# Reordering the first feed-forward groups of an encoder block, and its last stores

## The chip, the cores and the metric

One Trainium2 chip, one of its cores. The metric is the time of one execution on the device in microseconds, the median of several runs; lower is better. Five engines work side by side, each through its own instruction queue in order: PE (TensorE, matmuls), DVE (VectorE), ACT (ScalarE), POOL (GpSimd), and SP (SyncE), which here only issues DMA transfers. ACT also issues a few transfers.

## The reference

One layer of a hybrid encoder over 1024 tokens of width 1024, all in float32: an input LayerNorm, one wide projection, dilated attention and a bidirectional gated recurrence, their gated merge, and then the part that matters here.

```python
h = layer_norm(DEEPNORM_ALPHA * h + merged @ w_o[l], ln1_g[l], ln1_b[l])
gate, up = jnp.split(h @ w_ffn_in[l], 2, axis=-1)          # 1024 -> 2 x 2816
h = layer_norm(DEEPNORM_ALPHA * h + (jax.nn.silu(gate) * up) @ w_ffn_out[l], ln2_g[l], ln2_b[l])
```

## The kernel before

**Precision.** A float32 product is made of three matmuls (`mm3`): both factors are split into a high part (a rounding cast on ACT, L204) and a low part (the difference, on POOL or DVE, L208), and hi x hi, hi x lo and lo x hi are summed in PSUM (L229 to L231). A matmul on a weight block therefore needs a cast and a difference first; the split blocks (`w_hi`, `w_lo`) lie in a ring of four.

**Winograd-Strassen groups.** Products of the feed-forward part are computed in 2 x 2 blocks with seven block products instead of eight. Of the weights, the raw block columns `f_raw` hold a11, a12, a21, a22; s1 to s4 are sums of them. Of the activations, h is cut into blocks b11, b12, b21, b22 of 4 x 128 rows by 512 tokens; t1 to t4 are sums of them:

```python
PRODUCTS = {5: ("s1", "t1"), 1: ("a11", "b11"), 2: ("a12", "b21"), 6: ("s2", "t2"), 3: ("s4", "b22"),
            7: ("s3", "t3"), 4: ("a22", "t4")}
```

A group has one pair of raw blocks and seven products of 12 matmuls of 128x512 each. There are 22 groups; partial sums are kept by ACT (`wkeep`, "keep") or left in PSUM, and four evictions (`evac` in `ffn_in`) turn them into the tile `fc`: for the first row a DVE add (L1447), a tanh on ACT (L1448) and a DVE product (L1449).

**The passage from w_o to the groups (`phase2`).** Eight tiles of 128 tokens pass through w_o, in two halves of 512 columns each (`half(t, 0)`, `half(t, 1)`: 24 matmuls, then DVE's residual add L1227 into the row `y1` and its statistics). `norm` normalises the row (ACT, for tile 7 DVE L1239; the inverse root is a power on POOL, L1235). `turn(t)` transposes it on PE (L259), evicts it (`tsv`), makes the sums for the blocks (`h1_blocks`) and stores the row. Tiles 0 to 3 give b11 and b21; tiles 4 to 7 give t1 and t2, which stay on chip, and b22, t3 and t4, which DVE makes in `tsum` tiles and SP stores to the scratch `td` in memory (L1307) because their place is still taken. `ffn_in` loads those three "late blocks" from `td` (`t_raw`, L1504) and splits them, four pieces each.

From tile 7 to the end of the first two groups the order on every engine is written by hand: inside `in_order()` each instruction is bound behind the one emitted before it on its engine. The two first groups g0 and g1 run as generators (`wino_ahead`) that `phase2` and `ffn_in` advance in turns. Everything else is ordered by a planner that picks what is ready. On-chip memory of a closed pool is used again by later pools; an instruction that writes there waits for the last use of the tile that lay there.

**The output product (`ffn_out`).** The same seven products for `w_ffn_out`, with 11 block steps each; in the last product but one, p = 7, the activations `ghi`, `glo` (from scratch `gs3`) are loaded three steps ahead by SP, inside a hand-written order in which also the finished rows 0 to 3 are normalised (`whole`, `end`) and stored. Then the last product runs by token tile t = 0 to 3 over `a22h`, `a22l`, two tiles of which are loaded ahead and two when their buffers come free.

Of the kernel before, what the change touches and what calls it, by code (L numbers as in the profile page):

```python
# [10 lines left out]
F32 = mybir.dt.float32  # L11
# [3 lines left out]
OP = mybir.AluOpType  # L15
# [63 lines left out]
TABW = 128 * 5 + 64 + 256 + 384 + 256 + 192  # L79


class Block:
# [171 lines left out]
    def transposed(self, pool, n, q, g, b, v=None, bufs=2, on_act=(1, 3, 6)):  # L254
# [887 lines left out]
    def phase2(self):  # L1142
        nc = self.nc
        gc, bc = self.col["g1"], self.col["b1"]
        with ExitStack() as es:
# [56 lines left out]
            def load(t):  # L1202
                Y[t] = yp.tile([128, D], F32, name="y1", tag="y1", bufs=3)
                nc.sync.dma_start(Y[t], self.ahs_d[t])
# [45 lines left out]
            for t in range(7):  # L1250
# [11 lines left out]
                if t < 6:  # L1262
                    turn(t)()
# [5 lines left out]
            self.lasts = {}  # L1269
            with self.in_order():  # L1270
                half(7, 0)
                rest = turn(6)
                self.first_groups = [self.wino_ahead(raws[f], lambda *a, f=f: self.first_evac[f](*a), f)
                                     for f in range(2)]
# [16 lines left out]
    def h1_blocks(self, pool, t, v, last=False):  # L1291
# [9 lines left out]
        if t < 4:  # L1301
            for i, n in enumerate(("b11", "b21")):
                put(n, v(i))
            return lambda: None
# [18 lines left out]
        def rest():  # L1323
            nc.vector.tensor_sub(t2, b22, t1)
            put("t2", t2)
            t3 = tmp()
            nc.vector.tensor_sub(t3, b22, b12)
# [5 lines left out]
            nc.vector.tensor_add(t4, t4, lo)  # L1333
            later(2, "t4", t4)

        return rest

    def wino_a(self, A, name):

        nc = self.nc  # L1340
        how = {"s1": ("a21", "a22", OP.add, nc.vector), "s2": ("s1", "a11", OP.subtract, nc.vector),
               "s3": ("a11", "a21", OP.subtract, nc.gpsimd), "s4": ("a12", "s2", OP.subtract, nc.vector)}
        if name not in A:
            a, b, op, e = how[name]
            A[name] = o = A["sum"]()
            e.tensor_tensor(o, A[a], A[b], op)  # L1346
        return A[name]

    def wino_parts(self, raws, evac, swap):

        nc = self.nc
        A = {"sum": lambda: self.ws.tile([128, 4, 128], F32, name="wsum", tag="wsum", bufs=3)}
        for i, r in enumerate(raws):
            for j in range(2):
                A[f"a{i + 1}{j + 1}"] = r[:, 4 * j:4 * j + 4, :]
        banks, made = {}, {}

        def prep(n):
            hi, lo = made[n] = self.granules()
            self.split(hi, lo, self.wino_a(A, self.PRODUCTS[n][0]))  # L1360

        def product(n, bank, first):
            if n not in made:
                prep(n)
            hi, lo = made[n]
            xhi, xlo = self.xb[self.PRODUCTS[n][1]]
            if first:
                banks[bank] = self.ps_pj() if (bank == 2) != swap else self.ps_sd()
            ps = banks[bank]
            for k in range(4):  # L1370
                self.mm3(ps, hi[:, k, :], lo[:, k, :], xhi[:, k, :], xlo[:, k, :], first and k == 0, k == 3,
                         skip_group_check=True)
            return ps

        def keep(ps):
            with self.tc.high_priority(offset=self.evac_ahead):
                t = self.ws.tile([128, HALF], F32, name="wkeep", tag="wkeep", bufs=4)
                nc.scalar.copy(t, ps)
            return t

        def out(i, l, ps, add):
            with self.tc.high_priority(offset=self.evac_ahead):
                evac(i, l, ps, add)

        return prep, product, keep, out

    def wino_project(self, raws, evac):

        prep, product, keep, out = self.wino_parts(raws, evac, False)
        m5 = keep(product(5, 2, True))  # L1390
        yield
        m1 = keep(product(1, 1, True))
        out(0, 0, product(2, 3, True), m1)
        u2 = keep(product(6, 1, False))
        out(0, 1, product(3, 2, False), u2)
        out(1, 1, product(7, 1, False), m5)
        yield
        out(1, 0, product(4, 1, False), None)

    def wino_ahead(self, raws, evac, f):  # L1400

        prep, product, keep, out = self.wino_parts(raws, evac, f == 1)
        prep(1)
        prep(2)
        yield
        m1 = keep(product(1, 1, True))
        c11 = product(2, 3, True)
        prep(5)
        yield
        out(0, 0, c11, m1)  # L1410
        prep(6)
# [18 lines left out]
    def ffn_in(self):  # L1430

        nc = self.nc
        with ExitStack() as es:
# [75 lines left out]
            with self.in_order():  # L1509
# [8 lines left out]
                for f in splits[4:]:  # L1518
                    f()
# [359 lines left out]
```

## Time and profile before

| | us |
|---|---|
| median of 3 runs | 2172.78 |
| lowest and highest | 2172.17, 2176.0 |
| profiled execution, its own time | 2176.61 |
| span of that execution, first to last instruction | 2174.8 |
| PE busy | 2046.9 (94%) |
| DVE busy | 1392.7 (64%) |
| POOL busy | 1200.0 (55%) |
| ACT busy | 916.1 (42%) |

The page of the profile tells the busy time of each engine, the chain of work that ended last and the costliest groups of instructions. Other views of the trace list the instructions of one engine in order of time with the idle time before them in brackets and what ended it, or the busy time of all engines in stretches of the span. Lines are named by their line in the kernel (L208); `fc<-wkeep,sd` reads "writes `fc` from `wkeep` and `sd`", where `sd` and `pj` are PSUM banks. Times are counted from the start of the span.

### The profile page before, as it was taken

Reading aid. Unit: us, or ns where it says so; the run is one execution under the profiler, and the core shown is the slowest. Engines: PE = TensorE matmul, PEld = TensorE weight load, DVE = VectorE, ACT = ScalarE, POOL = GpSimd, SP = SyncE. Lnnn points to the kernel's source line nnn. Section 1 sums busy time; section 2 is a strip of 40 time slices with the busy share of each in tenths; the row PEclk is TensorE's granted clock in tenths of the full one; section 3 lists DMA queues with packets and bytes.
Section 4 is the critical chain, followed back from the end, with each engine's and each line's share of the span. In section 5 each row is a group of like instructions: output and inputs, shape, how many; then the busy total and the mean of one; then the engine's idle time right before and its main releaser. Section 6 shows DMA issues by size and latency. Waiting matters only on the chain. (4 is left out here: it accounts for less than half of the span.)

```text
span 2174.8 us, 31264 instructions
## 1 busy us (share of the span) xinstructions
PE 2046.9 (94%) x10941; PEld 1682.7 (77%) x10941; DVE 1392.7 (64%) x2172; ACT 916.1 (42%) x1867; POOL 1200.0 (55%) x955
## 2 busy tenths in 40 slices
PE   4799999999999999989999899996999999999987
PEld 3678887778878888778888688784788888888866
DVE  7667646876368845867455623445668787868645
ACT  6534455434544436344363421243444434344221
POOL 3565553566436764656545764232567776754552
PEclk9899999999999999999999999998999999999999
DMA  5343442435334352334526663434434454458664
GB/s 205 101 127 101 154 142 85 143 115 158 122 108 140 124 170 93 122 117 135 163 94 207 224 229 115 126 107 131 131 127 163 155 170 155 146 204 289 204 224 140
DMA packets 296447, 324.20 MB, mean 149 GB/s; under 512 B 15905, under 2 KB 212834, under 8 KB 296290
## 3 DMA queue, kind: packets, MB, share of 16 engines
q1 hardware_dynamic: 288832, 296.81, 42.3%
q10 hardware_dynamic: 7458, 25.40, 2.9%
q8 instruction: 86, 1.41, 0.3%
q14 instruction: 71, 0.58, 0.1%
HBM read 211.78 MB, written 110.36 MB: 148 GB/s over the span
## 5 line engine op out<-in xcount | busy, mean ns | idle before, releaser
L208 POOL TENSOR_TENSOR w_lo<-wa,w_hi 128x512 fp32r<-128x512 f32 x276 | 386.4, 1408 | 275.4 <-ACT w_hi L204 261.5
L204 ACT CAST w_hi<-wa 128x512 fp32r<-128x512 f32 x276 | 170.0, 618 | 231.7 <-PE pj L230 167.8
L208 POOL TENSOR_TENSOR w_lo<-wsum,w_hi 128x512 fp32r<-128x512 f32 x88 | 134.2, 1534 | 97.3 <-ACT w_hi L204 62.0
L208 POOL TENSOR_TENSOR w_lo<-f_raw,w_hi 128x512 fp32r<-128x512 f32 x66 | 108.5, 1656 | 69.7 <-ACT w_hi L204 66.1
L229 PE MATMUL pj<-xt1hi,w_hi 128*128 128x512 f32 x268 | 107.8, 403 | 12.6 <-ACT xt1hi L204 6.8
L230 PE MATMUL pj<-xt1lo,w_hi 128*128 128x512 f32 x268 | 106.6, 398 | 4.5 <-DVE xt1lo L208 4.5
L231 PE MATMUL pj<-xb22hi,w_lo 128*128 128x512 f32 x268 | 104.8, 391 | 1.9 <-POOL w_lo L208 1.9
L231 PE MATMUL pj<-xt1hi,w_lo 128*128 128x512 f32 x268 | 106.2, 396 | 0.0
L229 PE MATMUL pj<-xb22hi,w_hi 128*128 128x512 f32 x268 | 105.7, 394 | 0.0
L230 PE MATMUL pj<-xb22lo,w_hi 128*128 128x512 f32 x268 | 104.8, 391 | 0.0
L463 POOL TENSOR_TENSOR wa<-wa,wa 128x512 f32<-128x512 f32 x46 | 64.4, 1402 | 71.2 <-DVE ws L462 56.2
L208 POOL TENSOR_TENSOR w_lo<-Wb,w_hi 128x512 fp32r<-128x512 f32 x47 | 65.2, 1388 | 68.2 <-ACT w_hi L204 68.2
L208 POOL TENSOR_TENSOR w_lo<-ws,w_hi 128x512 fp32r<-128x512 f32 x46 | 67.3, 1466 | 63.1 <-ACT w_hi L204 60.9
L204 ACT CAST w_hi<-wsum 128x512 fp32r<-128x512 f32 x88 | 54.6, 621 | 74.1 <-PE sd L230 57.5
L485 ACT COPY wkeep<-pj 128x512 f32<-128x512 f32 x138 | 80.2, 581 | 11.4 <-DVE evh L377 5.9
L229 PE MATMUL pj<-xt2hi,w_hi 128*128 128x512 f32 x188 | 76.2, 406 | 8.5 <-ACT w_hi L204 8.5
L229 PE MATMUL pj<-xb11hi,w_hi 128*128 128x512 f32 x188 | 77.9, 416 | 5.2 <-DVE wkeep L402 3.0
L1448 ACT ACTIVATE fth<-fc 128x512 f32<-128x512 f32 x44 | 27.8, 632 | 126.4 <-DVE fc L1447 126.4
L388 DVE TENSOR_TENSOR evh<-wkeep,pj 128x512 f32<-128x512 f32 x48 | 32.7, 680 | 75.1 <-PE pj L231 54.8
L229 PE MATMUL pj<-xt4hi,w_hi 128*128 128x512 f32 x188 | 75.9, 404 | 4.0 <-DVE evh L377 4.0
L231 PE MATMUL pj<-xt2hi,w_lo 128*128 128x512 f32 x188 | 75.6, 402 | 3.7 <-POOL w_lo L208 3.5
L975 ACT ACTIVATE hS<-hR,dec 128x128 f32<-128x128 f32 x112 | 44.5, 402 | 79.8 <-DVE hR L984 57.2
(423 smaller groups left out, 6689.7 us busy)
## 6 DMA issues: line engine op xcount, KB each, us to landing
wa<-in_w_in_dram SPq DMA_DIRECT2D x184, 256.0 KB, 3.0
f_raw<-in_w_ffn_in_dram SPq DMA_DIRECT2D x44, 512.0 KB, 4.0
Wb<-in_w_ffn_out_dram SPq DMA_DIRECT2D x40, 256.0 KB, 5.2
tg<-evh SPq DMA_DIRECT2D x32, 256.0 KB, 3.2
tg<-tg SPq DMA_DIRECT2D x16, 512.0 KB, 4.0
y<-ahs SPq DMA_DIRECT2D x16, 512.0 KB, 5.9
ah<-xt ACTq DMA_DIRECT2D x8, 512.0 KB, 6.5
rec<-hg ACTq DMA_DIRECT2D x8, 512.0 KB, 3.9
```

Of the source, the lines that this page charges most:

```text
L204: nc.scalar.copy(hi, src)
L208: e.tensor_sub(lo, src, hi.bitcast(F32))
L229: nc.tensor.matmul(ps, whi, xhi, start=first, stop=False, **kw)
L230: nc.tensor.matmul(ps, whi, xlo, start=False, stop=False, **kw)
L231: nc.tensor.matmul(ps, wlo, xhi, start=False, stop=last, **kw)
L388: nc.vector.tensor_add(t, add, ps)
L463: nc.gpsimd.tensor_sub(a["a21"], a["a11"], a["a21"])
L485: nc.scalar.copy(t, ps)
L975: nc.scalar.activation(S[:, c, :], E, AF.Copy, scale=dec[:, 1, c:c + 1])
L1448: nc.scalar.activation(th[:, s], c[:, s], AF.Tanh, scale=0.5)
```

## The change

Five things change.

- The first two groups are objects of a class `Group` with single steps instead of generators. Weight blocks are prepared at least a product ahead: g0's s1, s2 and the splits for products 1 and 2 stand before w_o half (7, 0), g1's for 1 and 2 behind half (7, 1), and so on.
- `turn` now returns two parts. The second (t2) and the rest (b22, t3, t4) are placed separately: the rests of tiles 6 and 7 stand together behind g1's products 1 and 2.
- The late blocks are split at other places: b22 behind g1's product 6, t3 behind g0's product 3, t4 behind g1's product 3.
- Sums are made in place: s3 and s4 overwrite a11 and a12 in `f_raw`, t3 overwrites b12, t4 overwrites t2. `y1` has 2 buffers (3 before) and `tsv` 4 (2 before).
- In `ffn_out` the stores of finished rows are put in a list and issued in the loop of the last product, behind the loads for it.

The diff, cut to its core:

```diff
+class Group:
+    HOW = {"s1": ("a21", "a22", OP.add, "vector"), "s2": ("s1", "a11", OP.subtract, "vector"),
+           "s3": ("a11", "a21", OP.subtract, "gpsimd"), "s4": ("a12", "s2", OP.subtract, "vector")}
+    def sum(self, name):
+        if name not in A:
+            a, b, op, e = self.HOW[name]
+            if name in ("s1", "s2"):
+                A[name] = o.ws.tile([128, 4, 128], F32, name="wsum", tag="wsum", bufs=3)
+            else:
+                A[name] = A[a]
+            getattr(o.nc, e).tensor_tensor(A[name], A[a], A[b], op)
+        return A[name]
+    def first(self):
+        self.m1 = self.keep(self.product(1, 1, True))
+        self.c11 = self.product(2, 3, True)
+    ...
 # phase2
-                Y[t] = yp.tile([128, D], F32, name="y1", tag="y1", bufs=3)
+                Y[t] = yp.tile([128, D], F32, name="y1", tag="y1", bufs=2)
 ...
             with self.in_order():
+                g0.sum("s1")
+                g0.sum("s2")
+                g0.prep(1, 2)
                 half(7, 0)
-                rest = turn(6)
-                self.first_groups = [...]
-                next(self.first_groups[0])
+                second, rest = turn(6)
                 half(7, 1)
                 norm(7)
+                g1.prep(1, 2)
+                second()
+                g0.first()
+                second, last = turn(7)
+                g0.prep(5)
+                second()
+                g1.first()
+                g0.prep(6)
                 rest()
-                next(self.first_groups[0])
-                next(self.first_groups[1])
-                turn(7)()
+                last()
 # h1_blocks
-        def rest():
+        def second():
             nc.vector.tensor_sub(t2, b22, t1)
             put("t2", t2)
-            t3 = tmp()
-            nc.vector.tensor_sub(t3, b22, b12)
-            later(1, "t3", t3)
+        def rest():
             later(0, "b22", b22)
-            t4 = tmp()
+            nc.vector.tensor_sub(b12, b22, b12)
+            later(1, "t3", b12)
             hi, lo = (z[:, :, c].bitcast(F32) for z in self.xb["b21"])
-            nc.vector.tensor_sub(t4, hi, t2)
-            nc.vector.tensor_add(t4, t4, lo)
-            later(2, "t4", t4)
+            nc.vector.tensor_sub(t2, hi, t2)
+            nc.vector.tensor_add(t2, t2, lo)
+            later(2, "t4", t2)
 # ffn_in
             with self.in_order():
+                g0.out(0, 0, g0.c11, g0.m1)
+                g0.m5 = g0.keep(g0.product(5, 2, True))
+                g1.prep(5)
+                g0.u2 = g0.keep(g0.product(6, 1, False))
+                g1.out(0, 0, g1.c11, g1.m1)
+                g1.prep(6)
                 splits = late_block(0)
-                next(g1)
+                g1.m5 = g1.keep(g1.product(5, 2, True))
+                g0.prep(3)
                 splits += late_block(1)
-                next(g0)
+                g1.u2 = g1.keep(g1.product(6, 1, False))
                 for f in splits[:4]:
                     f()
-                next(g1)
-                nxt = self.ffn_raws(FS[2])
+                g0.prep(7)
+                g0.out(0, 1, g0.product(3, 2, False), g0.u2)
                 for f in splits[4:]:
                     f()
+                g1.prep(3)
                 splits = late_block(2)
-                next(g0)
+                g0.out(1, 1, g0.product(7, 1, False), g0.m5)
+                g1.prep(7)
+                g1.out(0, 1, g1.product(3, 2, False), g1.u2)
+                g0.prep(4)
                 for f in splits:
                     f()
-                next(g1)
-                next(g0, None)
+                nxt = self.ffn_raws(FS[2])
+                g1.out(1, 1, g1.product(7, 1, False), g1.m5)
+                g0.out(1, 0, g0.product(4, 1, False), None)
 # ffn_out
             def end():
                 t = ends.pop(0)
                 nc.vector.tensor_add(Y[t], Y[t], V[1])
-                store(t)
+                stores.append(t)
 ...
                     if t < 2:
                         for i in range(2):
                             last_acts(2 + t, i)
+                    while stores:
+                        store(stores.pop(0))
```

More of the change, by code (lines that the diff above doesn't have):

```diff
@@ L79, with __init__, prep, product @@
 TABW = 128 * 5 + 64 + 256 + 384 + 256 + 192
+class Group:
+    HOW = {"s1": ("a21", "a22", OP.add, "vector"), "s2": ("s1", "a11", OP.subtract, "vector"),
+           "s3": ("a11", "a21", OP.subtract, "gpsimd"), "s4": ("a12", "s2", OP.subtract, "vector")}
+    def __init__(self, block, raws, swap=False):
+        self.o, self.swap, self.evac = block, swap, None
+        self.A = {f"a{i + 1}{j + 1}": r[:, 4 * j:4 * j + 4, :] for i, r in enumerate(raws) for j in range(2)}
+        self.banks, self.made = {}, {}
+    def sum(self, name):
+        A, o = self.A, self.o
+        if name not in A:
[6 more added lines that the diff above has]
+        return A[name]
+    def prep(self, *ns):
+        for n in ns:
+            hi, lo = self.made[n] = self.o.granules()
+            self.o.split(hi, lo, self.sum(self.o.PRODUCTS[n][0]))
+    def product(self, n, bank, first):
+        o = self.o
+        if n not in self.made:
+            self.prep(n)
+        hi, lo = self.made.pop(n)
+        xhi, xlo = o.xb[o.PRODUCTS[n][1]]
+        if first:
+            self.banks[bank] = o.ps_pj() if (bank == 2) != self.swap else o.ps_sd()
+        ps = self.banks[bank]
+        for k in range(4):
+            o.mm3(ps, hi[:, k, :], lo[:, k, :], xhi[:, k, :], xlo[:, k, :], first and k == 0, k == 3,
+                  skip_group_check=True)
+        return ps
+    def keep(self, ps):
+        o = self.o
+        with o.tc.high_priority(offset=o.evac_ahead):
+            t = o.ws.tile([128, HALF], F32, name="wkeep", tag="wkeep", bufs=4)
+            o.nc.scalar.copy(t, ps)
+        return t
+    def out(self, i, l, ps, add):
+        with self.o.tc.high_priority(offset=self.o.evac_ahead):
+            self.evac(i, l, ps, add)
+    def first(self):
+        self.m1 = self.keep(self.product(1, 1, True))
+        self.c11 = self.product(2, 3, True)
+    def steps(self, evac):
+        self.evac = evac
+        self.m5 = self.keep(self.product(5, 2, True))
+        yield
+        self.first()
+        self.out(0, 0, self.c11, self.m1)
+        self.u2 = self.keep(self.product(6, 1, False))
+        self.out(0, 1, self.product(3, 2, False), self.u2)
+        self.out(1, 1, self.product(7, 1, False), self.m5)
+        yield
+        self.out(1, 0, self.product(4, 1, False), None)
@@ L1262, in phase2 @@
                 if t < 6:
-                    turn(t)()
+                    for f in turn(t):
+                        f()
                 else:
@@ L1303, in h1_blocks @@
                 put(n, v(i))
-            return lambda: None
+            return ()
         def later(i, name, v):
@@ L1336, in h1_blocks @@
[L1336 to L1411, printed above, removed]
-        m5 = keep(product(5, 2, True))
-        u2 = keep(product(6, 1, False))
-        prep(3)
-        prep(7)
-        yield
-        out(0, 1, product(3, 2, False), u2)
-        out(1, 1, product(7, 1, False), m5)
-        yield
-        out(1, 0, product(4, 1, False), None)
+            nc.vector.tensor_sub(t2, hi, t2)
@@ L1422, in ffn_raws @@
+            nc.vector.tensor_add(t2, t2, lo)
+            later(2, "t4", t2)
+        return second, rest
     def ffn_raws(self, f):
@@ L1736, in whole @@
                     end()
-            ends = []
+            ends, stores = [], []
             def end():
```

13 lines of the change are left out of this document (7 added, 6 removed).

## The prediction

> **What bounds the kernel now.** I read the stages of TensorE first (busy time of each engine in stretches), then who TensorE waited for, then the order of time of each engine where it waits.
>
> ```profile
> 1388.30:1476.40 88.10, 86.82 (x409) 71.50 (x407) 45.11 (x95) 35.98 (x65) 28.27 (x29) 1.00 0.36 113
> 1476.40:1546.50 70.10, 46.40 (x152) 34.21 (x152) 36.30 (x57) 24.71 (x48) 19.07 (x15) 0.81 0.36 117
> 1546.50:1934.00 387.50, 386.69 (x1692) 316.55 (x1692) 307.19 (x288) 162.97 (x288) 279.19 (x175) 1.00 0.47 155
> 2104.00:2130.00 26.00, 13.26 (x36) 9.57 (x36) 12.76 (x21) 8.77 (x11) 16.59 (x11) 0.74 0.40 142
> ```
>
> Columns: stretch, length, busy time of PE, PEld, DVE, ACT, POOL, granted clock, DMA share, GB/s. The w_o halves before 1476 and the feed-forward loop after 1546 are full of matmuls: time saved ahead of the loop stays saved. TensorE is short of work in two places, the first groups (1476 to 1546) and the end of `ffn_out` (from 2104). The change touches both. What TensorE waits for in the first place, and the speed at which it resumes:
>
> ```profile
> 1479.65 0.50 PE L229 MATMUL sd<-xb11hi,w_hi 128*128 128x512 f32 x1 [3.34 <-ACT w_hi L204]
> 1492.08 0.79 PE L231 MATMUL pj<-xb11hi,w_lo 128*128 128x512 f32 x1 [1.83 <-POOL w_lo L208]
> 1505.69 0.80 PE L229 MATMUL sd<-xt2hi,w_hi 128*128 128x512 f32 x1 [4.27 <-ACT w_hi L204]
> 1511.05 0.63 PE L231 MATMUL sd<-xt2hi,w_lo 128*128 128x512 f32 x1
> 1511.48 0.63 PE L229 MATMUL sd<-xt1hi,w_hi 128*128 128x512 f32 x1
> 1523.11 0.79 PE L229 MATMUL pj<-xt2hi,w_hi 128*128 128x512 f32 x1 [8.45 <-ACT w_hi L204]
> 1534.05 0.50 PE L229 MATMUL sd<-xt3hi,w_hi 128*128 128x512 f32 x1 [2.14 <-ACT xt3hi L204]
> 1546.50 0.50 PE L229 MATMUL sd<-xt4hi,w_hi 128*128 128x512 f32 x1 [1.25 <-ACT w_hi L204]
> ```
>
> The brackets are idle time. Matmuls start 0.43 us apart behind the longer pauses (1511.05, 1511.48); in the loop one takes 386.69 / 1692 = 0.228. Twelve products and one set of transposes are 12 x 12 x 0.228 + 1.0 = 33.9 us of full-speed work; they lie between 1476.3 and 1545.25, 68.9 us. So 35 us are to be had: 23.7 idle by the stage's row, the rest slow clock.
>
> **The change, part by part.** *Weights a product ahead.* The casts of g0's products 1 and 2 move ahead of w_o half (7,0), so g0's first 24 matmuls follow half (7,1) at 1476.3 and end at 1481.8. Tile 7's transposes are next, and they need its normalised row:
>
> ```profile
> 1470.88 0.68 DVE L1227 SCALAR_TENSOR_TENSOR y<-pj,y 128x512 f32<-128x512 f32 x1
> 1478.33 0.68 DVE L1227 SCALAR_TENSOR_TENSOR y<-pj,y 128x512 f32<-128x512 f32 x1
> 1479.73 2.51 POOL L208 TENSOR_TENSOR w_lo<-f_raw,w_hi 128x512 fp32r<-128x512 f32 x2 [13.52 <-ACT w_hi L204]
> 1480.02 0.15 DVE L1234 TENSOR_SCALAR mv<-mv 128x1 f32<-128x1 f32 x1
> 1482.19 0.55 POOL L1235 TENSOR_TENSOR mv<-mv,mhalf 128x1 f32<-128x1 f32 x1
> 1482.78 1.00 DVE L1239 TENSOR_SCALAR y<-y,mv 128x512 f32<-128x512 f32 x2 [2.61 <-POOL mv L1235]
> 1464.84 1.03 PE L259 MATMUL sd<-tabs_sb,y 128*128 128x128 f32 x8
> y<-ahs SPq DMA_DIRECT2D x8, 512.0 KB, 5.9
> ```
>
> The power on POOL stood behind the two w_lo of g0; these are now done earlier, so it starts at 1480.2 and not 1482.19. Against that stands `y1` with 2 buffers: tile 7's row can only be loaded when tile 5's transposes have read theirs (1465.87), and lands 0.3 + 5.9 us later, at 1472.1 or sooner; its use at 1470.88 slips by about 0.9 (0 if the load is faster). Half (7,1) is then evicted at 1479.2, the power ends at 1481.7, the row at 1482.7, the transposes at 1483.9, and g1's 24 matmuls, whose weights were prepared in the meantime, at 1489.3. The waits of 3.34 and 1.83 and the slow stretches behind them are gone. The other deeper or shallower rings (`tsv`, `tsum`) cost nothing: tile 7's slots were last used for tile 5's sums and tile 6's first one, which are done by then.
>
> *Late sums of tile 6 behind tile 7's.* This is where the next wait arises:
>
> ```profile
> 1488.45 1.37 DVE L269 TENSOR_SCALAR tsv<-sd,vc 128x128 f32<-128x128 f32 x4 [0.15 <-PE sd L259]
> 1496.05 0.69 DVE L208 TENSOR_TENSOR xt2lo<-tsum,xt2hi 128x512 fp32r<-128x512 f32 x1 [0.69 <-ACT xt2hi L204]
> 1496.66 0.69 DVE L1327 TENSOR_TENSOR tsum<-tsv 128x512 f32<-128x512 f32 x1
> 1497.98 0.69 DVE L1333 TENSOR_TENSOR tsum<-tsum,xb21lo 128x512 f32<-128x512 f32 x1
> 1502.25 0.69 DVE L1447 TENSOR_TENSOR fc<-wkeep,sd 128x512 f32<-128x512 f32 x1 [2.98 <-DMA td<-tsum]
> ```
>
> g0's first eviction (`fc`) waits until tile 7's last sum t4 has been stored, because `fc` is laid where `tsum` was; 3.6 us pass from that sum's end to `fc`. The order after keeps this wait and puts six sums, not three, ahead of it. DVE after 1482.7: tile 6's t2 pair as before (2.0), tile 7's evictions to xt2lo 1488.45 to 1496.74, of which I take 7.6 (POOL runs against it for less of the time), six sums at 2.0 for three: 1496.4; `fc` at 1500.0. In the DVE order g1's s1 stands behind this `fc`, and so do s2 and all later sums; ACT's tanh stands there too, ahead of g1's casts. From `fc` to the first matmul on the sum's cast took 1502.25 to 1505.69, 3.44. So g1's product 5 starts at 1503.4. TensorE covers until about 1497 with g0's products 5 and 6 (their own short waits are swallowed by this): 6.4 idle, then 1.3 for w_lo and ten matmuls at 0.43, to 1508.8. Product 6 follows without a wait, to 1511.6: the 8.45 is gone.
>
> *Late blocks behind the sixth products.*
>
> ```profile
> 1511.72 0.59 ACT L1378 COPY wkeep<-sd 128x512 f32<-128x512 f32 x1 [5.59 <-PE sd L231]
> L1448 ACT ACTIVATE fth<-fc 128x512 f32<-128x512 f32 x44 | 27.8, 632 | 126.4 <-DVE fc L1447 126.4
> 1515.97 2.17 ACT L204 CAST xb22hi<-t_raw 128x512 fp32r<-128x512 f32 x4
> 1535.44 0.50 PE L230 MATMUL sd<-xt3lo,w_hi 128*128 128x512 f32 x1 [0.88 <-DVE xt3lo L208]
> 1532.86 4.08 DMA f_raw<-in_w_ffn_in_dram
> ```
>
> The b22 casts stand on ACT behind the keep of g1's product 6, so they cannot hide: keep 0.6 and first cast 0.6 give 1.4 idle with the hand-overs, and the DVE parts pace the product (0.7 for the first, 0.65 for each block); it ends at 1516.3 and not at 1514.3. The blocks' loads go out behind the last td stores, at about 1497, and are first used at 1512, so g1's products 5 and 6 cover them. The t3 casts stand behind the tanh of that product (`fc` 0.7, tanh 0.6, cast 0.6): 2.0 idle and 0.8 for the first low part, the figure that the old wait of 2.14 and 0.88 had. A slow stretch follows as it did then; product 7 ends at 1523.4, g1's product 3 at 1526.2, and its product 7, with 0.5 for w_lo (s3, cast and w_lo now serial behind POOL's previous w_lo), at 1529.4. The old time is 1545.25: 15.8 us. s3 and s4 now overwrite `f_raw`, so the load for the third group waits for the last w_lo and not for the sum, then 4.08 and the s1, cast and w_lo chain: I take 2.0 of idle for the old 1.25 (between 0, if g1's product 4 fills it, and 4). First groups: 15.1 gained.
>
> *The clock, by row and by page.* The old pause of 2.14 + 0.88 was enough for the slow clock. The Trainium skill, "TensorE: Matmul & The Clock Gate", Part 1, says that the clock halves after at least one idle window of about 3.4 us; no such window fits into that pause, so the trace disagrees. By this page of the Trainium skill the t3 pause and the longer a22 pause below would cost no clock, and the sum would be 2.6 us better (eight matmuls at 0.2 here, 1.0 there). I go by the row.
>
> *Stores behind loads.* At the end of `ffn_out`:
>
> ```profile
> 2113.27 1.71 POOL L208 TENSOR_TENSOR w_lo<-Wb,w_hi 128x512 fp32r<-128x512 f32 x1
> 2114.54 0.77 PE L229 MATMUL pj<-w_hi,ghi 128*128 128x512 f32 x1 [7.04 <-DMA ghi<-gs3h]
> 2115.10 0.73 PE L230 MATMUL pj<-w_lo,ghi 128*128 128x512 f32 x1
> 2116.84 4.75 SPq L1728 DMA_DIRECT2D out_dram<-y  x2
> 2123.99 1.71 POOL L208 TENSOR_TENSOR w_lo<-Wb,w_hi 128x512 fp32r<-128x512 f32 x1
> 2125.38 0.77 PE L229 MATMUL pj<-w_hi,ghi 128*128 128x512 f32 x1 [5.46 <-DMA ghi<-gs3h]
> 2151.27 0.77 SPq L1676 DMA_DIRECT2D a22l<-ga22l  x1
> 2159.75 0.50 PE L231 MATMUL pj<-t4hi,a22l 128*128 128x512 f32 x1 [0.96 <-DMA a22l<-ga22l]
> 2143.00:2150.00 7.00, 7.00 (x32) 5.81 (x31) 1.98 (x6) 1.24 (x1) 2.94 (x2) 1.00 0.77 205
> 2163.00:2167.00 4.00, 4.00 (x18) 3.03 (x17) 0.47 (x1) 0.00 (x0) 0.00 (x0) 1.00 0.33 131
> ```
>
> The waits of 7.04 and 5.46 are put down to loads behind a store on SP. But the second matmul needs w_lo, which POOL finishes at 2114.98 and 2125.70, behind the row products that the change leaves in place; it started at 2115.10 and 2125.95. The loads come early now, the waits stay; gain 0.3. The four stores go out behind the a22 loads of the third tile, so ahead of those of the fourth. A pair of a22 loads takes 0.77 x 7 = 5.4 us of all DMA engines, a store 0.33 x 4 = 1.3, four 5.3: they keep the engines until about 2155, where the last a22 pair began at about 2152. Landing slips by 0 to 3, I take 2.3; the pause of 0.96 becomes 3.3 and can bring a slow stretch (ten matmuls, up to 2; I take 1.0). Cost 3.3 (0 to 5), net 3.0. The Trainium skill, "DMA: Bandwidth & Descriptors", section "Queues, rings and completion order", says that each engine takes descriptors of a ring in order, which speaks against this part; by it the slip is the full 3.
>
> **Sum.** 2176.6 - 15.1 + 3.0 = 2164.5 in the profiled execution's own time (span 2174.8 and 1.8 around it). That execution is 3.8 above the median of 2172.8, so 2172.8 - 12.1 = 2160.7.
>
> **Rivals.** (a) `fc` falls on a slot of `tsum` whose store is done: DVE goes straight on, 3.6 earlier: 2157.1. For it: the ring is now used in another order. Against: the third and the second slot both lie under `fc`. (b) The stores run beside the a22 loads, which wait no longer than now: 2157.4. (c) Pauses of 2 to 3 us keep the full clock: 2.6 less, 2158.1; the row of 2.14 speaks against it. This is what the Trainium skill, "TensorE: Matmul & The Clock Gate", Part 1, would make of them. (d) Tile 7's load is queued on SP behind tile 5's t4 store, which the sum at DVE sets (1476.4): it lands at 1482.9, ten later, and DVE with it: 2170.7. For it: one SP queue; against: before, the queue ran loads ahead of sums not yet made. (e) Slower: two `y1` buffers hold every w_o row. From a tile's transposes to the next use of its buffer there are about 5 us (1465.87 to 1470.88) for a load of 5.9; if an eviction that is 3 late held TensorE in each of six tiles it would cost 18, less the net 12.1: 2179. It decides from 2.8 a tile on. Against: four banks turn over (`pj`, 0 to 3), so TensorE runs three halves ahead.
>
> **How the numbers follow.** A few executions tell about 0.2% (4.3 us) from no change. Forecast 0.52 (0.04 of it within 0.2%), (a) 0.12, (b) 0.13, (c) 0.06, (d) 0.11, (e) 0.06. Faster 0.79, same 0.15, slower 0.06. The range adds the bounds: gain of the first groups 11 to 19, end of `ffn_out` -0.3 to 5: 2154 to 2168. The forecast's own range is 2156 to 2166.
>
> **What would show it.** Right: g0's product 1 at about 1476 without a wait; one idle time of 5 to 8 us ahead of g1's product 5, `fc` waiting for a td store; idle times of 1 to 3 ahead of the products on b22 and t3; idle times of 7 and 5.5 near 2110 and 2120 put down to w_lo; a longer wait on a22l. Wrong: w_o evictions waiting for row loads, tile 7's transposes late by over 2, or no wait at `fc`.

## The result, and the profile after

| | before | after |
|---|---|---|
| median, us (5 runs each, same chip) | 2176.00 | 2163.86 |
| lowest and highest | 2172.17, 2179.19 | 2162.12, 2164.29 |
| profiled execution, its own time | 2176.61 | 2162.12 |
| its span | 2174.8 | 2160.2 |

The ratio of after to before is 0.9943, 95% interval 0.9927 to 0.9959: faster by 12.1 us. Forecast: 2160.7 from a median of 2172.8, a ratio of 0.9944. The kernel before had a median of 2176.0 in these runs, and against it the forecast drop of 12.1 us is what was measured. The parts of the drop are not what was forecast, so that the agreement of the totals is luck; the parts come first.

Both kernels issue 10,941 matmuls, in the same order but for a few neighbours. So the time between the n-th and the m-th matmul can be compared stretch by stretch, without the differences that pile up ahead of it. All stretches below are worked out so from the traces of the profiled executions. The first columns are this one pair; the last is the spread over the kernels below that are alike in the part concerned, with their count.

| stretch (from, to matmul) | before | after | difference | over all profiles |
|---|---|---|---|---|
| up to w_o (start of the span to 7720) | 1380.78 | 1380.58 | -0.20 | 1377.3 to 1387.2; the instructions are the same |
| w_o (7720 to 8160) | 95.15 | 93.83 | -1.32 | see the fifth experiment |
| first groups (8160 to 8380) | 86.05 | 74.48 | -11.57 | 85.6 to 86.1 (2); 74.1 to 74.9 (4) |
| loop (8380 to 10660) | 521.46 | 518.46 | -3.00 | sums in a third buffer 521.1 to 521.7 (3), in place 518.2 to 519.6 (10) |
| end of `ffn_out` (10660 to 10940) | 83.25 | 84.74 | +1.49 | mean with stores ahead of the loads 83.2 (7), behind them 85.3 (5) |

The terms forecast were -15.1 for the first groups, 0 for w_o and loop, +3.0 for the end: each is off, by amounts that in part cancel.

In the first groups, TensorE's rows with idle time in brackets, in order of time, for the kernel after from g1's product 5 on (in this kernel the matmuls of `mm3` are L297 to L299, casts L272, low parts L276). Ahead of them no idle time is longer than 1.07:

```profile
1503.41 0.80 PE L297 MATMUL sd<-xt1hi,w_hi 128*128 128x512 f32 x1 [5.63 <-ACT w_hi L272]
1513.25 0.51 PE L297 MATMUL pj<-xb22hi,w_hi 128*128 128x512 f32 x1 [1.25 <-ACT xb22hi L272]
1513.97 0.50 PE L298 MATMUL pj<-xb22lo,w_hi 128*128 128x512 f32 x1 [0.22 <-DVE xb22lo L276]
1518.72 0.50 PE L297 MATMUL sd<-xt3hi,w_hi 128*128 128x512 f32 x1 [1.95 <-ACT xt3hi L272]
1519.54 0.79 PE L298 MATMUL sd<-xt3lo,w_hi 128*128 128x512 f32 x1 [0.32 <-DVE xt3lo L276]
...
1530.46 0.50 PE L298 MATMUL sd<-xt4lo,w_hi 128*128 128x512 f32 x1 [0.38 <-DVE xt4lo L276]
1533.98 0.50 PE L298 MATMUL sd<-xt4lo,w_hi 128*128 128x512 f32 x1 [1.86 <-DVE xt4lo L276]
1547.62 0.50 PE L299 MATMUL pj<-xb22hi,w_lo 128*128 128x512 f32 x1 [0.84 <-POOL w_lo L276]
```

The waits of 3.34, 4.27 and 8.45 of before are gone; one long idle time is left, ahead of g1's product 5. DVE's order says what it hangs on:

```profile
1479.20 2.91 DVE L1307 TENSOR_SCALAR y<-y,mv 128x512 f32<-128x512 f32 x2 [0.73 <-POOL mv L1303]
...
1495.60 0.69 DVE L1409 TENSOR_TENSOR tsum<-tsum,xb21lo 128x512 f32<-128x512 f32 x1
1499.98 0.69 DVE L1439 TENSOR_TENSOR fc<-wkeep,sd 128x512 f32<-128x512 f32 x1 [3.69 <-DMA td<-tsum]
...
1532.63 0.69 DVE L100 TENSOR_TENSOR wsum<-f_raw 128x512 f32<-128x512 f32 x1 [1.62 <-DMA f_raw<-in_w_ffn_in_dram]
1533.24 1.28 DVE L276 TENSOR_TENSOR xt4lo<-t_raw,xt4hi 128x512 fp32r<-128x512 f32 x2
```

Row 1 was not forecast: the two halves of tile 7's row took 1.00 before and take 2.91. Row 3 is the forecast wait: 3.69 behind tile 7's last sum, for its store. Rows 4 and 5 explain the 1.86 at 1533.98: between the second and the third low part of t4 stands the third group's first weight sum, whose load is not there yet.

At the end of `ffn_out`, TensorE's idle times and SP's order:

```profile
2095.81 0.59 PE L297 MATMUL pj<-w_hi,ghi 128*128 128x512 f32 x1 [3.85 <-ACT w_hi L272]
2098.96 0.80 PE L298 MATMUL pj<-w_lo,ghi 128*128 128x512 f32 x1 [2.56 <-POOL w_lo L276]
2106.56 0.80 PE L297 MATMUL pj<-w_hi,ghi 128*128 128x512 f32 x1 [2.99 <-ACT w_hi L272]
2109.71 0.80 PE L298 MATMUL pj<-w_lo,ghi 128*128 128x512 f32 x1 [2.36 <-POOL w_lo L276]
2128.21 6.01 SPq L1734 DMA_DIRECT2D out_dram<-y  x4
2134.32 1.10 SPq L1682 DMA_DIRECT2D a22h<-ga22h  x1
2135.51 1.79 SPq L1682 DMA_DIRECT2D a22l<-ga22l  x1
2142.91 0.47 PE L297 MATMUL pj<-t4hi,a22h 128*128 128x512 f32 x1 [0.92 <-DMA a22h<-ga22h]
2145.16 0.50 PE L299 MATMUL pj<-t4hi,a22l 128*128 128x512 f32 x1 [1.54 <-DMA a22l<-ga22l]
```

The loads of `ghi` are early now, and TensorE still waits 6.41 and 5.35 in two pieces, for w_hi and w_lo. Behind four stores the last a22 pair is late by 0.92 and 1.54.

### The profile page after: what moved, and what is told of

The parts are those of the page before. It is cut to its first block, busy times and chain, and to the rows that moved or that the text cites. A ratio compares the mean times of both kernels' runs of the same rounds, so it can differ in the third digit from the quotient of the medians.

```text
span 2160.2 us, 31223 instructions
## 1 busy us (share of the span) xinstructions
PE 2038.3 (94%) x10941; PEld 1678.3 (78%) x10941; DVE 1368.7 (63%) x2172; ACT 918.3 (43%) x1867; POOL 1199.0 (56%) x955
## 4 chain that ended last, share of the span: by engine, by line
PE 60%; DVE 6%; issue 5%; POOL 4%; DMA 2%; ACT 2%; SPq 0%; DVEq 0%; POOLq 0%; ACTq 0%
PE pj L297 13%; PE pj L298 12%; PE pj L299 12%; PE sd L297 6%; PE sd L298 6%; PE sd L299 5%; POOL w_lo L276 2%; PE sd L1091 1%; ACT p L869 1%; DVE hR L1052 1%; PE sd L905 1%; DVE p L891 1%; DVE hR L1051 1%; DMA a22l<-ga22l 0%; PE sd L696 0%
## 5 line engine op out<-in xcount | busy, mean ns | idle before, releaser
L276 POOL TENSOR_TENSOR w_lo<-wa,w_hi 128x512 fp32r<-128x512 f32 x276 | 386.7, 1409 | 277.0 <-ACT w_hi L272 255.1
L272 ACT CAST w_hi<-wa 128x512 fp32r<-128x512 f32 x276 | 170.1, 618 | 230.1 <-PE pj L298 162.3
L276 POOL TENSOR_TENSOR w_lo<-f_raw,w_hi 128x512 fp32r<-128x512 f32 x110 | 175.7, 1609 | 112.9 <-ACT w_hi L272 51.0
L297 PE MATMUL pj<-xt1hi,w_hi 128*128 128x512 f32 x268 | 108.6, 406 | 15.1 <-ACT xt1hi L272 6.6
L299 PE MATMUL pj<-xt1hi,w_lo 128*128 128x512 f32 x268 | 106.7, 398 | 0.7 <-POOL w_lo L276 0.7
L299 PE MATMUL pj<-xb22hi,w_lo 128*128 128x512 f32 x268 | 104.9, 392 | 2.4 <-POOL w_lo L276 2.4
L297 PE MATMUL pj<-xb22hi,w_hi 128*128 128x512 f32 x268 | 105.7, 394 | 1.2 <-ACT xb22hi L272 1.2
L276 POOL TENSOR_TENSOR w_lo<-Wb,w_hi 128x512 fp32r<-128x512 f32 x47 | 66.2, 1410 | 68.0 <-ACT w_hi L272 63.7
L272 ACT CAST w_hi<-f_raw 128x512 fp32r<-128x512 f32 x110 | 67.9, 620 | 83.0 <-DVE f_raw L100 32.5
L276 POOL TENSOR_TENSOR w_lo<-ws,w_hi 128x512 fp32r<-128x512 f32 x46 | 67.3, 1468 | 63.0 <-ACT w_hi L272 60.8
L276 POOL TENSOR_TENSOR w_lo<-wsum,w_hi 128x512 fp32r<-128x512 f32 x44 | 65.9, 1498 | 34.2 <-ACT w_hi L272 33.7
L297 PE MATMUL pj<-xb11hi,w_hi 128*128 128x512 f32 x188 | 77.0, 411 | 4.9 <-DVE wkeep L470 3.3
L297 PE MATMUL pj<-xt4hi,w_hi 128*128 128x512 f32 x188 | 75.5, 402 | 2.9 <-DVE evh L445 2.9
L299 PE MATMUL pj<-xt2hi,w_lo 128*128 128x512 f32 x188 | 74.3, 395 | 3.4 <-POOL w_lo L276 3.4
L298 PE MATMUL pj<-xb11lo,w_hi 128*128 128x512 f32 x188 | 75.6, 402 | 1.0 <-DVE xb11lo L276 1.0
L530 DVE TENSOR_TENSOR ws<-wa,wa 128x512 f32<-128x512 f32 x46 | 38.5, 838 | 60.0 <-DMA wa<-in_w_in_dram 44.5
```

The costliest lines, as they stand in the source:

```text
L272: nc.scalar.copy(hi, src)
L276: e.tensor_sub(lo, src, hi.bitcast(F32))
L297: nc.tensor.matmul(ps, whi, xhi, start=first, stop=False, **kw)
L298: nc.tensor.matmul(ps, whi, xlo, start=False, stop=False, **kw)
L299: nc.tensor.matmul(ps, wlo, xhi, start=False, stop=last, **kw)
L530: nc.vector.tensor_add(a["s1"], a["a21"], a["a22"])
```

## The experiments

Ratios are to the kernel before, measured on the same chip in the same job.

**1. Another slot for `fc`, first try.** After, with the two `fc` tiles made in the other order:

```diff
-            self.first_evac = [evac_of(FS[p]) for p in range(2)]
+            self.first_evac = [evac_of(FS[p]) for p in (1, 0)][::-1]
```

> The changed kernel with one edit: the result tiles of the first two groups are taken in the other order, so that g1's fc and not g0's lies where the tsum tiles lay. Theory (the 5.6 us idle time ahead of g1's product 5 comes from g0's first eviction, which waits for the td store of tile 7's t4 only because its fc overlaps that tsum tile): fc of g0 starts right behind the last sum, about 3.7 us earlier, the idle time falls from 5.6 to about 2, g1's first eviction now has the DMA wait in front of it (about 1 us), kernel 3 to 4 us faster than the changed one. Rival (the wait would come anyway, by the store itself or by the next thing behind it on DVE): idle time above 4.5, gain below 1.

Measured: 2164.97, ratio 0.9944 (0.9927 to 0.9960); `fc` still waits, DVE's row reads:

```profile
1502.51 0.69 DVE L1439 TENSOR_TENSOR fc<-wkeep,sd 128x512 f32<-128x512 f32 x1 [3.68 <-DMA td<-tsum]
```

This tells nothing of the theory. In the laid-out program g0's `fc` has the address that it had, 120800, over the `tsum` slots at 119264 and 121312: in both layouts the tile that is written first got that place, though the two were made in the other order. The edit did not change what it was meant to change.

**2. `fc` off the slots, second try.** The late sum's tile `fu`, first used near 1524, is laid at the low end of the pool, and `fc` 4 KB higher:

```diff
             self.fp = fp = es.enter_context(self.pool("ffn", "right"))
+            fp.tile([128, HALF], F32, name="fu", tag="fu", bufs=2)
```

> The changed kernel, with the tile of the late sum (fu) put at the low end of the feed-forward pool, where it is first used some 20 us later; fc and fth move up by 4 KB and fc no longer lies over any slot of tsum. Theory: g0's fc waited (3.69 us, DMA td<-tsum) only because of what lay under it. Then DVE goes from tile 7's last sum (ending 1496.3) straight to fc, g1's product 5 starts about 3.7 us earlier (1503.4 to 1499.8), the idle time ahead of it falls from 5.6 to about 2, and the kernel takes 2160.2 instead of 2163.9. Rival: the next thing that is late takes it back, the blocks b22, t3 and t4 or the third group's f_raw load: the wait is gone, the loop starts less than 1 us earlier, and the time is within 1.5 us of the changed kernel's 2163.9.

Measured: 2160.65 (2159.22 to 2162.75), ratio 0.9927 (0.9914 to 0.9941). DVE, then TensorE ahead of g1's product 5:

```profile
1496.27 0.69 DVE L1409 TENSOR_TENSOR tsum<-tsum,xb21lo 128x512 f32<-128x512 f32 x1
1496.88 0.68 DVE L1440 TENSOR_TENSOR fc<-wkeep,sd 128x512 f32<-128x512 f32 x1
...
1500.32 0.50 PE L297 MATMUL sd<-xt1hi,w_hi 128*128 128x512 f32 x1 [1.88 <-ACT w_hi L272]
```

The wait is gone, the idle time 1.88 where it was 5.63, and the first groups take 70.33 where they took 74.48: 4.15 less, all of it kept up to the loop. By time alone the kernel is not clear of the one after, whose interval is 0.9927 to 0.9959; the stretch shows the gain, since the four kernels alike in this part lie between 74.1 and 74.9. The theory holds, and so does the forecast's price for its first rival (3.6 earlier), which lacked only its condition, an `fc` off the busy slots. The rival here, that a later wait takes the gain back, falls.

**3. g1's weights behind tile 7's row.**

```diff
-                g1.prep(1, 2)
                 second()
+                g1.prep(1, 2)
```

> The changed kernel, with g1's weights 1 and 2 prepared behind tile 7's normalisation instead of ahead of it. Theory: DVE's two y operations took 2.91 us instead of 1.00 because POOL made two w_lo (2.70) at the same time on the port that they share. With the order turned round they take 1.0 again, tile 7's transposes start 1.5 to 2 us earlier, fc and g1's product 5 move with them, and the kernel takes 2162 to 2162.5. Rival 1: w_lo is now late for g1's products 1 and 2, and TensorE waits there by as much as it gained: time unchanged within 0.5. Rival 2: y stays at 2.9, since something else slows it, and nothing moves before the transposes.

Measured: 2160.47 (2159.77 to 2165.74), ratio 0.9931 (0.9919 to 0.9944). Beside the row of 2.91 at 1479.20, shown above, POOL had this in the kernel after:

```profile
1479.13 2.70 POOL L276 TENSOR_TENSOR w_lo<-f_raw,w_hi 128x512 fp32r<-128x512 f32 x2
```

With the edit, DVE, POOL and TensorE:

```profile
1477.22 1.00 DVE L1307 TENSOR_SCALAR y<-y,mv 128x512 f32<-128x512 f32 x2 [0.73 <-POOL mv L1303]
1480.12 2.52 POOL L276 TENSOR_TENSOR w_lo<-f_raw,w_hi 128x512 fp32r<-128x512 f32 x2 [2.94 <-ACT w_hi L272]
...
1480.05 0.50 PE L297 MATMUL pj<-xb11hi,w_hi 128*128 128x512 f32 x1 [0.91 <-ACT w_hi L272]
```

With POOL out of the way the row takes 1.00 again: theory right on the cause, rival 2 out. The first groups gain 0.97 (73.51, where the four kernels alike take 74.1 to 74.9), not 1.5 to 2: TensorE now waits 0.91 for w_hi, and POOL's w_lo slow a DVE sum instead (1.68 for 0.69 at 1481.51). So rival 1 holds by half. By stretches the edit is worth 1 us. The median is 3.4 lower than after's, but from another set of runs; in the profiled execution the stretch up to w_o, where nothing was edited, was 2.4 shorter than in after's.

**4. Weights ahead, alone, on the kernel before.**

```diff
-                half(7, 0)
-                rest = turn(6)
                 self.first_groups = [...]
                 next(self.first_groups[0])
+                half(7, 0)
+                rest = turn(6)
```

> The kernel before, with one part of the change alone: the weights of g0's products 1 and 2 are prepared ahead of the w_o half (7,0). Theory: the wait of 3.34 us ahead of g0's product 1 goes, the power on POOL no longer stands behind two w_lo and ends 2 us earlier, tile 7's row and fc with it, so that g1's product 5 starts about 2 us earlier; the waits of 8.45 and 2.14 behind it stay as long as they were, and the kernel takes 2 to 3 us less (ratio 0.9986 to 0.9991). Rival: the wait of 3.34 is hidden by the chain of DVE up to fc, which does not move, and the time stays within 0.5 us.

Measured: 2174.43, ratio 0.9991 (0.9983 to 1.0000), too close to 1 to tell by time. The stretch tells: the first groups take 84.83 for 86.05, 1.2 less; `fc` comes 1.2 earlier, counted from the 8160th matmul. So of the 11.6 us, this part alone brings about 1.2 (expected 2 to 3): the 3.34 goes, and the waits behind it grow or stay:

```profile
1486.68 0.80 PE L229 MATMUL pj<-xb11hi,w_hi 128*128 128x512 f32 x1 [4.96 <-ACT w_hi L204]
...
1520.92 0.79 PE L229 MATMUL pj<-xt2hi,w_hi 128*128 128x512 f32 x1 [8.44 <-ACT w_hi L204]
```

The rest of the gain comes from the new order of sums, products and late blocks taken together with it; which of these gives how much was not measured one by one.

**5. Two `y1` buffers, alone, on the kernel before** (`bufs=3` to `bufs=2`).

> The kernel before, with one part of the change alone: two y1 buffers in place of three. Theory: a third row load no longer stands on SP ahead of the first w_o weight blocks, so that they land earlier; the two waits of 0.83 and 0.45 us at the start of w_o go and the w_o stage starts 1.3 us earlier, while the rest stays: from the end of the phases before w_o to the first groups 1.3 to 1.5 us less, the total at a ratio of 0.9994. Rival: the 1.5 us came from the order of the changed w_o stage; then the waits stay, and in the w_o halves the smaller ring costs 0 to 3 us a tile.

Measured: 2175.15, ratio 0.9990 (0.9981 to 1.0000); w_o takes 93.99 for 95.15. But two other kernels with three buffers (experiments 4 and 6) have 94.40 and 94.78 there, and those with two 93.83 to 94.59. So the rings explain at most some half a microsecond of the 1.32, and the rest is what one execution differs from the next: the two idle times at the start of w_o, 0.66 and 0.53 before, are absent after, but 0.53 stands there again in experiment 10, with two buffers. The theory, that the smaller ring removes them, is not shown. The smaller ring costs nothing: that rival, and the forecast's rival (e), are out.

**6. Sums in place, alone, on the kernel before.**

```diff
-            A[name] = o = A["sum"]()
+            A[name] = o = A["sum"]() if name in ("s1", "s2") else A[a]
```

> The kernel before, with one part of the change alone: the weight sums s3 and s4 are written over the raw block instead of into a third buffer. Theory: this part makes the loop's gain of 3.0 us (0.3 us at every second group, at product 2, where w_lo was late); the loop takes 3.0 us less, the first groups stay within 1 us, and the time falls by 3 us, to a ratio of 0.9986. Rival: the loop's gain comes from the order in which the engines enter it, which the first groups set; then the loop is as before, and the third group's raw load, which now waits for the last reader of the block, can cost up to 4 us: ratio 1.000 to 1.002.

Measured: 2173.59, ratio 0.9991 (0.9981 to 1.0001). The loop takes 519.12 for 521.46, 2.3 less. From the 8450th to the 10060th matmul it keeps pace with the kernel after to 0.01 us, while before loses 2.74 there, 0.3 at every second group. So the loop's gain is this part's. The first groups lose 1.06 (87.11), so that the total is not told from no change. Where it acts is seen in who POOL waits for between 1600 and 1900, the two largest sums each, first before, then with this edit, then after:

```profile
POOL w_lo L208 <- ACT w_hi L204: 55.8, 32, 3.5
POOL w_lo L208 <- PE sd L231: 27.4, 9, 3.5
```

```profile
POOL w_lo L208 <- DVE s L1489: 35.4, 8, 4.5
POOL w_lo L208 <- ACT w_hi L204: 34.4, 25, 2.8
```

```profile
POOL w_lo L276 <- DVE s L1481: 36.0, 8, 4.5
POOL w_lo L276 <- ACT w_hi L272: 33.0, 23, 3.0
```

(Columns: us in total, times, longest.) The second and the third are alike and the first is not: in place, POOL's work in the loop falls in another order, and w_lo for product 2 is no longer the last to arrive. That the order, and not the freed buffer itself, does it is my reading of these rows; it was not tested apart.

**7. Blocks b22 and t3 split early.** On after, b22's four splits go ahead of g1's product 6 and t3's, with g1's weights for product 3, ahead of g0's product 3:

```diff
-                g1.u2 = g1.keep(g1.product(6, 1, False))
                 for f in splits[:4]:
                     f()
+                g1.u2 = g1.keep(g1.product(6, 1, False))
                 g0.prep(7)
-                g0.out(0, 1, g0.product(3, 2, False), g0.u2)
+                g1.prep(3)
                 for f in splits[4:]:
                     f()
-                g1.prep(3)
+                g0.out(0, 1, g0.product(3, 2, False), g0.u2)
```

> The changed kernel with the splits of b22 put ahead of the keep of g1's product 6, and those of t3 (and the preparation of g1's product 3) ahead of g0's eviction of product 3. Theory (the idle times on b22 and t3 come from the place of the splits on ACT behind a keep and a tanh that wait for TensorE): idle times of 1.25 + 0.2 and 1.95 + 0.3 fall to below 1 together, no slow stretch in product 7, kernel 4 to 6 us faster than the changed one. Rival (DVE and ACT are the limit there, and the work only changes places): new waits on w_hi or w_lo of products 7 and 3 of 3 us or more, gain below 2.

Measured: 2166.27, ratio 0.9946 (0.9931 to 0.9961), first groups 75.28 against 74.48: no gain. DVE's row for b22 in the kernel after:

```profile
1513.23 2.50 DVE L276 TENSOR_TENSOR xb22lo<-t_raw,xb22hi 128x512 fp32r<-128x512 f32 x4 [6.76 <-ACT xb22hi L272]
```

With the edit, DVE's rows for the two blocks, and TensorE's waits on t4:

```profile
1510.03 5.37 DVE L276 TENSOR_TENSOR xb22lo<-t_raw,xb22hi 128x512 fp32r<-128x512 f32 x4 [4.14 <-ACT xb22hi L272]
1517.26 4.24 DVE L276 TENSOR_TENSOR xt3lo<-t_raw,xt3hi 128x512 fp32r<-128x512 f32 x4 [1.26 <-ACT xt3hi L272]
1531.61 0.49 PE L298 MATMUL sd<-xt4lo,w_hi 128*128 128x512 f32 x1 [1.49 <-DVE xt4lo L276]
1535.58 0.50 PE L298 MATMUL sd<-xt4lo,w_hi 128*128 128x512 f32 x1 [1.85 <-DVE xt4lo L276]
```

After, b22's four low parts took 2.50; here they meet POOL's sums and w_lo and take 5.37. The work changed its place: TensorE now waits for the low parts of b22 and t3 instead of their casts, and on t4 it waits 1.49 and 1.85 where it was 0.38 and 1.86. The rival was right that nothing is gained; the waits of 3 us on w_hi or w_lo that it named did not come.

**8. Stores where they were.** After, with each finished row stored at once:

```diff
-                stores.append(t)
+                store(t)
```

> The changed kernel with the stores of the finished rows issued in end() again, as before the change. Theory (the two idle times in p = 7 are set by POOL's w_lo, the stores only move bytes in front of the last a22 loads): p = 7 ends at the same distance from the loop within 0.5 us, with idle times put down to ghi loads again; the waits on a22 fall from 0.9 + 1.5 to about 1.0 in all; 1.5 us faster than the changed kernel. Rival (stores ahead of loads on SP cost time): p = 7 gets longer by 2 us or more and the kernel is slower.

Measured: 2163.27, ratio 0.9935 (0.9920 to 0.9950), in total not told from after. The end of `ffn_out` takes 82.41 for 84.74, and the idle times are those of before:

```profile
2101.32 0.77 PE L297 MATMUL pj<-w_hi,ghi 128*128 128x512 f32 x1 [6.78 <-DMA ghi<-gs3h]
2112.28 0.77 PE L297 MATMUL pj<-w_hi,ghi 128*128 128x512 f32 x1 [5.90 <-DMA ghi<-gs3h]
2145.84 0.50 PE L299 MATMUL pj<-t4hi,a22l 128*128 128x512 f32 x1 [0.22 <-DMA a22l<-ga22l]
```

12.7 us wait here under the name of a load and 11.8 wait after under the names of w_hi and w_lo, and from the 10720th to the 10900th matmul it is 58.85 against 58.05: the loads were late and it hardly mattered. Over all profiles the stretch on a22 (10900 to 10940) is 9.6 to 10.4 with the stores ahead and 11.2 to 12.1 with them behind the loads.

**9. Stores behind the very last loads.** After, with `while t and stores` for `while stores`, so that the four stores follow the fourth tile's a22 loads.

> The changed kernel with the four stores issued behind the loads for the last token tile as well (one pass of the loop later). Theory (the stores share the DMA engines with the last a22 pair): both a22 waits go (below 0.5 together), 2 us faster than the changed kernel. Rival (the a22 pair is slow by itself, because its buffers come free too late): about 1.0 of wait stays, as before the change, 1.5 us faster; if the stores then run into the last rows' stores the end gets later by up to 3.

Measured: 2165.19, ratio 0.9939 (0.9919 to 0.9959). The a22 stretch falls to 10.10, 1.97 less than after's: it was the four stores. Nine stores then stand at the end, `2141.45 19.95 SPq L1734` by SP's row, and from the start of the last matmul to the end of the span it is 8.10 us, as before (8.09), so they cost nothing there. But the stretch ahead of it took 74.14, 1.5 longer than after's 72.67, which is within the 72.4 to 74.4 of the other profiles; in total the time is not told from after's.

**10. The best together:** edits 2, 3 and 8 on the kernel after.

> The changed kernel with three of the single steps together: fc away from tsum's slots, g1's weights 1 and 2 behind tile 7's normalisation, and the out stores in their old place. Theory: the three act in different places and add up: 4.1 and 1.0 us in the first groups and 2.3 at the end of ffn_out, by the traces of the single runs; 2163.9 - 7.4 = 2156.5, a ratio to the kernel before of 0.9908. Rival: the first two gains are the same time, since both shorten DVE's way to fc and TensorE needs until about 1497 for g0's products anyway; then they give 4.2 together and the time is 2157.5 or more.

Measured: 2159.05 (2155.35 to 2163.43), ratio 0.9917 (0.9905 to 0.9930): the lowest median, and a ratio 0.0026 below that of after, with intervals that just overlap (0.9930 and 0.9927). That it beats experiment 2 alone (0.9927) is not shown by times. First groups 69.69 (4.79 less than after, 5.12 were expected), end of `ffn_out` 83.78 (0.96 less, where the one profile of experiment 8 had promised 2.3).

**11. t4's splits ahead of g1's product 3 as well,** on top of experiment 10:

```diff
+                for f in splits:
+                    f()
                 g1.out(0, 1, g1.product(3, 2, False), g1.u2)
                 g0.prep(4)
-                for f in splits:
-                    f()
```

> The kernel with the three steps together, and with block t4's splits ahead of g1's product 3 instead of behind it. Theory: the waits of 1.87 and 0.35 us on xt4lo come from the third group's first weight sum, which waits on DVE for its load (1.62 us, DMA f_raw) between the second and the third low part; with the splits ahead they go, and the loop starts 1.5 to 2.2 us earlier: 2154.5. Rival: the same wait on the f_raw load moves to TensorE's next product on those weights, or the splits hold up ACT's and DVE's evictions ahead of them: no difference to the three steps within 0.5 us, as when the blocks b22 and t3 were split early.

Measured: 2160.93, ratio 0.9924 (0.9911 to 0.9938), first groups 72.55 against 69.69. TensorE:

```profile
1524.48 0.49 PE L297 MATMUL sd<-xt4hi,w_hi 128*128 128x512 f32 x1 [1.54 <-ACT w_hi L272]
1525.76 0.50 PE L297 MATMUL pj<-xt1hi,w_hi 128*128 128x512 f32 x1 [0.56 <-ACT w_hi L272]
1527.41 0.76 PE L297 MATMUL pj<-xt4hi,w_hi 128*128 128x512 f32 x1 [0.78 <-DVE fu L1447]
```

The waits on xt4lo (2.21 in experiment 10) are gone, and ACT's weight casts, queued behind the splits and a tanh, are late in their place; behind the first two of the three pauses the clock is halved from 1526.19 to 1533.02. That is the rival, and worse than it. But of the 2.86 us between the two profiles 1.15 lie ahead of t3's product, where the edit does not act yet, so at most some 1.7 is the edit's.

## Why the prediction came out, point by point

**Weights a product ahead.** g0's product 1 follows w_o without a wait, as forecast. Tile 7's row was forecast to end at 1482.7, behind an eviction 0.9 late and with 1.00 of work of its own. Nothing was late, and the power on POOL ended at 1479.16, 2.5 ahead of the forecast (w_o had ended 1.5 earlier); yet the row ended only at 1482.11, since the two w_lo that the change put behind the power run beside the row and make it 2.91. This is the mis-sized term, 1.9 us on DVE's way to `fc`; experiment 3 shows the cause and that 1.0 of it comes back. The Trainium skill, "SBUF — State Buffer", section "SBUF: two separate sides", says that DVE and GpSimd share a pair of ports that one of them holds for a whole instruction. By that rule the row waits for w_lo, and the traces agree: 2.91 beside w_lo, 1.00 twice without (experiments 3 and 4). Tile 7's load was issued at 1464.42 and made no delay: rival (d) is out. The forecast's own slip for it, which its figures put at 1.2 (1472.1 less 1470.88) and its sum at 0.9, did not come either.

**Late sums behind tile 7's.** The step is right in kind and size: 3.69 for 3.6 behind the sum, 5.63 of idle for 6.4, g1's product 5 at 1503.41 for 1503.4. The start is exact by chance: w_o was 1.5 ahead, and the row 1.9 late. That it is the slot is shown by experiment 2, not only argued.

**Late blocks.** b22: 1.25 idle and a low part of 0.22 for a forecast of 1.4 and a pacing of some 0.65 a block that did not come; t3: 1.95 and 0.32 for 2.0 and 0.8, with the slow clock behind it. Product 7 ended at 1529.7 (forecast 1529.4): against w_o's end that is 14.0 gained for 15.8.

**Entry to the loop.** Forecast: 2.0 of idle for the old 1.25, a loss of 0.75. Found: from 14.0 to 11.57, a loss of 2.5. The size of the wait on the third group's load was right (1.86 on TensorE, 1.62 on DVE), but it is paid in the middle of t4's splits, and 0.38 ahead of it and 0.84 on w_lo at 1547.62 come on top.

**The loop.** Forecast as nothing; it gave 3.0. I had costed the in-place sums at their load only and did not ask whether the loop, whose groups make the same sums, would change: a row of 0.3 on w_lo stood in the trace before, repeated every second group.

**Stores.** The two long waits stayed, as forecast, though each is in two pieces: 2.56 and 2.36 are on w_lo, as forecast, and the longer 3.85 and 2.99 ahead of them on w_hi, ACT's cast, which the forecast did not name. The price behind the four stores was 2.46 of idle in two pieces (0.92 and 1.54) with no slow clock behind it; I had 3.3 in one. The stretch on a22 cost 1.7 in this pair and some 1.5 over all profiles. Rival (b), no cost, is out (experiments 8 and 9). The Trainium skill, "DMA: Bandwidth & Descriptors", section "Queues, rings and completion order", has each engine take a ring's descriptors in order; experiment 9 agrees in kind, since the wait goes when the loads are issued first. Its full 3 us of slip was too much: the idle time on a22 rose by 1.5, from 0.96 to 2.46.

**Sum.** -11.6, -3.0, -1.3 and -0.2, +1.5 is -14.6 for this pair of profiles. Forecast was -12.1, and the medians say -12.1. The terms are off by 3.5 too much gain in the first groups, 3.0 and 1.3 of gain in the loop and w_o that were put at nothing, and 1.5 too much cost at the end: that the forecast meets the medians to 0.1 us is luck, while the order of the waits was foreseen. The profiled pair lies 2.4 us further apart than the medians, since the profiled execution after is the fastest of its five (2162.12 for a median of 2163.86) and that before lies 0.6 above its median; in which stretches the other executions differ is not known. What of the -1.3 is due to the change is open.

## What to carry to other kernels

When one engine's order is written by hand, look at what lies under each tile that it writes: a tile laid over one that is still being stored turns a free instruction into a wait for a DMA and everything queued behind it, and here moving the tile by 4 KB was worth 4.15 us, two reorderings 0.97 and 1.2. Work that is moved earlier meets other work: what POOL does beside DVE belongs into the price, and after each move ask which queue the moved instructions now stand in front of. Compare stretches by counted instructions, not totals, when one execution differs from the next by more than the edit is worth; and read a wait's name as the last of several reasons only.

## What the runs showed of the hardware

**DVE beside POOL.** Operations of DVE on full 128x512 tiles took up to three times as long when POOL worked at the same time: the row 2.91 for 1.00, b22's low parts 5.37 for 2.50, single sums 1.68 to 1.78 for 0.69. Not every operation did: in the kernel after, beside POOL's three w_lo from 1535.64 to 1540.79, `fc<-fth,fu` took 1.78, with both inputs in SBUF, and `fc<-fth,sd`, which reads a PSUM bank, 0.67.

**The clock.** One and the same pause, 1.95 and 0.32 ahead of t3's product, brought the slow clock in the kernel after and none in experiment 10, TensorE's rows first after, then there:

```profile
1520.14 0.63 PE L299 MATMUL sd<-xt3hi,w_lo 128*128 128x512 f32 x1
1520.56 0.63 PE L297 MATMUL sd<-xt3hi,w_hi 128*128 128x512 f32 x1
```

```profile
1520.39 0.50 PE L297 MATMUL sd<-xt3hi,w_hi 128*128 128x512 f32 x1 [1.95 <-ACT xt3hi L272]
1521.21 0.50 PE L298 MATMUL sd<-xt3lo,w_hi 128*128 128x512 f32 x1 [0.32 <-DVE xt3lo L276]
1521.54 0.39 PE L299 MATMUL sd<-xt3hi,w_lo 128*128 128x512 f32 x1
1521.77 0.42 PE L297 MATMUL sd<-xt3hi,w_hi 128*128 128x512 f32 x1
```

Matmuls are 0.43 apart in the first, 0.23 in the second. The granted clock that the traces recorded says why. In each of the 13 traces it changes only at times that lie whole multiples of 3.41 us apart, and where these edges fall in the kernel differs from one execution to the next. The slices of 3.41 us around the pause, first after, then in experiment 10 (length, busy time of PE, PEld, DVE, ACT, POOL, granted clock, DMA share, GB/s):

```profile
1515.81:1519.22 3.41, 1.46 (x6) 0.64 (x4) 1.72 (x3) 1.69 (x4) 1.06 (x1) 1.00 0.81 252
1519.22:1522.63 3.41, 3.09 (x8) 2.48 (x8) 2.68 (x5) 1.63 (x3) 0.00 (x0) 0.50 0.54 164
```

```profile
1516.43:1519.84 3.41, 2.01 (x9) 1.30 (x7) 1.62 (x3) 1.13 (x3) 1.53 (x1) 1.00 0.80 238
1519.84:1523.25 3.41, 2.55 (x10) 1.85 (x11) 3.39 (x6) 2.06 (x4) 0.00 (x0) 1.00 0.76 223
```

After, the whole pause of 1.95 lies in one slice, and the next slice has half the clock. In experiment 10 an edge cuts the pause: the two slices have 1.40 and 0.86 of idle, and the clock stays. So it is with the 0.92 and 1.54 on a22 after, which fall into slices with 1.17 and 1.30 of idle. From 1300 us on, over all 13 traces, each of the 83 slices behind which the clock was halved had at least 1.51 of its 3.41 us idle, and of the 3064 slices behind which it stayed full none had more than 1.87; between these two figures both are seen. What decides here is the idle share of a slice, and so the length of a pause together with its place among the edges.

The Trainium skill, "TensorE: Matmul & The Clock Gate", Part 1, asks for an idle window of about 3.4 us; the 1.95 after, and the 1.54 and 0.56 of experiment 11, 2.10 in one slice, halved the clock without one, so the measurement decides against it as a condition. The forecast's rival (c) is out for its part on t3 in this execution and came true for its part on a22, where no slow clock followed.
